# Two of a kernel's first loads issued from ScalarE's queue, and the constants issued behind the third k-tile

## The chip, the cores and the metric

The kernel runs on one core of a Trainium2 chip. The metric is the device time of one execution in microseconds (us). Five engines run side by side: TensorE (PE; its weight loads are listed apart as PEld), VectorE (DVE), ScalarE (ACT), GpSimd (POOL) and SyncE (SP). Loads from the chip's memory into the tiles are carried out by 16 DMA engines; an instruction on some engine's queue issues each load, and in the kernel before all of them stand on SP's queue.

## The reference: what is computed

One decoder layer on 256 positions of width 1024, in float32. What matters here is its first step, a product of the input with one wide weight matrix:

```python
proj = x @ w_in[l]
q = proj[..., 0:a].reshape(bsz, s, N_HEADS, HEAD_DIM)
k = proj[..., a:2 * a].reshape(bsz, s, N_HEADS, HEAD_DIM)
v = proj[..., 2 * a:3 * a].reshape(bsz, s, N_HEADS, HEAD_DIM)
...
y_att = moba_attention(q, k, v) @ w_attn_out[l]
y_cnv = (gate_b * causal_dwconv(gate_c * h_in, conv_w_mix[l])) @ w_conv_out[l]
mix = (g_att * y_att + g_cnv * y_cnv) @ w_o[l]
x = layer_norm(DEEPNORM_ALPHA * x + mix, ln1_g[l], ln1_b[l])
u = causal_dwconv(x @ w_up[l], conv_w_ffn[l])
f = (jax.nn.silu(u[..., :D_FF]) * u[..., D_FF:]) @ w_down[l]
x = layer_norm(DEEPNORM_ALPHA * x + f, ln2_g[l], ln2_b[l])
```

With a = 512, q, k and v are the first 1536 columns of `proj`.

## The kernel before

**The weights come in chunks.** All matrices are packed on the host into one array, `wpack`, in the order in which they are used. A chunk is a tile of 128 partitions and up to 2048 columns, called `raw0`, `raw1` and so on. The first eight chunks are the eight k-tiles of the first product: k-tile k holds 128 rows of the transposed input (256 columns) and the same 128 rows of q's, k's and v's weights (512 columns each), 1792 columns in all, or 896 KB.

**The first two k-tiles are loaded in pieces** (line 53). The text calls them by the number of the tile and a letter:

- 0a is columns 0 to 512 of `raw0`: the input and the first half of q's weights, 256 KB.
- 0b is columns 512 to 1280: the second half of q's weights and all of k's, 384 KB.
- 0c is columns 1280 to 1792: v's weights, 256 KB.
- 1a is columns 0 to 768 of `raw1`: the input and all of q's weights, 384 KB.
- 1b is columns 768 to 1792: k's and v's weights, 512 KB.

All later chunks are loaded whole. `issue_dma(c)` issues every chunk up to c that isn't issued yet.

**The order is written out by hand.** Each engine runs its instructions in the order in which the program names them. On SP stand `issue_dma(1)` (the five pieces), then the load of `consts` (81 KB: positions, convolution taps and the norm's columns), then `issue_dma(EARLY - 1)` with whole chunks from `raw2` on. The first chunks have tiles of their own; from `raw7` on a load reuses a tile, and waits until that is read.

**Each product is made of three matmuls in float32r.** A chunk's piece, once loaded, is split into a high part (`wh`, a copy by ScalarE, helper line 258, or line 222 later) and a low part (`wl`, a subtraction by VectorE, lines 255, 259 and 236); the input is split in the same way into `xT`. TensorE then multiplies high by high, low by high and high by low. K-tile 0 begins with the first half of q's columns (`first_q`, line 676, matmuls of 256 columns), so that it needs 0a alone; then come the second half of q, then k (both from 0b) and v (from 0c); then q of k-tile 1 (from 1a), its k and v (from 1b), and so on. Ahead of it TensorE runs 31 matmuls on constants (`warm_up`). VectorE reads `consts` for the first time in `rope_tables` (line 325). `neghalf2`, a tile of one column, is allotted at line 283; before its first real use it only receives one ACTIVATE at line 1003, far behind.

Of the kernel before, what the change touches and what calls it, by code (L numbers as in the profile page):

```python
# [8 lines left out]
F32 = mybir.dt.float32  # L9
# [4 lines left out]
AF = mybir.ActivationFunctionType  # L14
ALU = mybir.AluOpType

P = 128
# [33 lines left out]
CHUNK = 2048  # L51

PIECES = {0: (0, 512, 1280, 1792), 1: (0, 768, 1792)}
OFF_B, OFF_C, OFF_H, OFF_G = 3 * AW, 3 * AW + CW, 3 * AW + 2 * CW, 3 * AW + 3 * CW
TAIL = 8

# [73 lines left out]
def transfers(chunks, units):  # L130

    out, at = [], 0
    for c, us in enumerate(chunks):
        end = units[us[-1]][1] + units[us[-1]][2] * units[us[-1]][3]
        cuts = PIECES.get(c, (0, end))
        assert cuts[-1] == end
# [8 lines left out]
def layer_kernel(ctx: ExitStack, tc: tile.TileContext, x, wpack, cpack, b_gate, ln1_g, ln1_b, ln2_g, ln2_b, out):  # L145
    nc = tc.nc

    cst = ctx.enter_context(tc.tile_pool(name="cst", bufs=1))
# [8 lines left out]
    def acc_bank(name):  # L157
        return psum.tile([P, 512], F32, tag="acc", name=name)
# [20 lines left out]
    def issue_dma(c):  # L179
        nonlocal ln2  # L180
        while len(raws) <= c and len(raws) < len(chunks):
            i = len(raws)
            if i in RAW_HOMES:
                t = big.tile([P, CHUNK], F32, tag=RAW_HOMES[i], name=f"raw{i}")
            else:
                t = wp.tile([P, CHUNK], F32, tag="raw", name=f"raw{i}", bufs=RAW_BUFS)
            raws.append(t)
            for a, b, off in blocks[i]:
                nc.sync.dma_start(t[:, a:b], wpack[off:off + P * (b - a)].rearrange("(p n) -> p n", p=P))
            if i == LN2_CHUNK:  # L190
                ln2 = big.tile([P, 2, D], F32, tag="e8", name="ln2")
                for j, g in enumerate((ln2_g, ln2_b)):
                    nc.sync.dma_start(ln2[:, j, :], bass.AP(tensor=g.tensor, offset=g.offset, ap=[[0, P], [1, D]]))
# [19 lines left out]
    def split_start(u):  # L213
        issue_dma(units[u]["chunk"] + RAW_BUFS - 1)
        alloc(u, "h", "wh")
        alloc(u, "l", "wl")
        return units[u]["h"], units[u]["l"]

    def split_h(u):
        issue_dma(units[u]["chunk"] + RAW_BUFS - 1)  # L220
        alloc(u, "h", "wh")
        nc.scalar.activation(units[u]["h"], raw_of(u), AF.Copy)  # L222
# [36 lines left out]
        (eng or nc.vector).tensor_tensor(l, src, h.bitcast(F32), op=ALU.subtract)  # L259


    issue_dma(1)
    warm = acc_bank("warm")

# [15 lines left out]
    PCOL = [slice(0, 128), slice(128, 384)]  # L280
    neghalf = cst.tile([P, 1], F32, name="neghalf")
    nc.gpsimd.memset(neghalf, -0.5)
    neghalf2 = cst.tile([P, 1], F32, name="neghalf2")
    invf = cst.tile([P, 8], F32, name="invf")
    for i, f in enumerate(INV_FREQ):
        nc.gpsimd.memset(invf[:, i:i + 1], f)


    consts = cst.tile([P, 162], F32, name="consts")
    nc.sync.dma_start(consts, cpack)  # L290
    posi = consts[:, 144:146].bitcast(I32)
# [1045 lines left out]
    for k in range(TAIL):  # L1337
        i = NP - TAIL + k
# [116 lines left out]
```

## Time and profile before

| What | us |
|---|---|
| Median of 3 runs (lowest 350.74, highest 351.62) | 351.54 |
| The profiled execution's own time | 350.94 |
| Its span, first to last instruction | 349.2 |
| PE busy | 342.3 (98%) |
| DVE busy | 300.8 (86%) |
| ACT busy | 256.3 (73%) |
| POOL busy | 7.8 (2%) |

Busy times are those of the profiled execution, shares are of its span. The chain of work that ended last is 94% PE.

### The profile page before, as it was taken

Reading aid. Unit: us, or ns where it says so; the run is one execution under the profiler, and the core shown is the slowest. Engines: PE = TensorE matmul, PEld = TensorE weight load, DVE = VectorE, ACT = ScalarE, POOL = GpSimd, SP = SyncE. Lnnn points to the kernel's source line nnn. Section 1 sums busy time; section 2 is a strip of 40 time slices with the busy share of each in tenths; the row PEclk is TensorE's granted clock in tenths of the full one; section 3 lists DMA queues with packets and bytes.
Section 4 is the critical chain, followed back from the end, with each engine's and each line's share of the span. In section 5 each row is a group of like instructions: output and inputs, shape, how many; then the busy total and the mean of one; then the engine's idle time right before and its main releaser. Section 6 shows DMA issues by size and latency. Waiting matters only on the chain.

```text
span 349.2 us, 4612 instructions
## 1 busy us (share of the span) xinstructions
PE 342.3 (98%) x1577; PEld 283.9 (81%) x1577; DVE 300.8 (86%) x528; ACT 256.3 (73%) x396; POOL 7.8 (2%) x27
## 2 busy tenths in 40 slices
PE   9999999999999999999999999999999999999993
PEld 7888888888888888888888888888888888888882
DVE  4897759999998999799879999899799969597975
ACT  4776979599987857779786788977688867677600
POOL 1000002010000000000000000000000000000001
PEclk9999999999999999999999999999999999999999
DMA  7995985896848787993599759886887867795003
GB/s 267 424 396 207 237 285 206 127 330 206 276 103 349 282 315 213 289 343 97 134 353 237 233 190 213 238 315 160 293 282 266 280 179 261 178 374 154 0 16 105
DMA packets 58343, 82.17 MB, mean 235 GB/s; under 512 B 47824, under 2 KB 48336, under 8 KB 51280
## 3 DMA queue, kind: packets, MB, share of 16 engines
q1 hardware_dynamic: 58320, 81.88, 74.3%
q8 instruction: 12, 0.20, 0.2%
q14 instruction: 11, 0.09, 0.1%
HBM read 69.29 MB, written 1.05 MB: 201 GB/s over the span
## 4 chain that ended last, share of the span: by engine, by line
PE 94%; DVE 1%; DMA 1%; SPq 1%; issue 1%; POOL 0%; POOLq 0%; DVEq 0%; ACT 0%
PE u L342 10%; PE u L341 10%; PE u L340 10%; PE qk L660 6%; PE d L342 5%; PE d L341 5%; PE d L340 5%; PE g L340 4%; PE g L341 4%; PE g L342 4%; PE u L1198 3%; PE v L660 3%; PE y L340 2%; PE y L342 2%; PE y L341 2%; PE o L340 2%
## 5 line engine op out<-in xcount | busy, mean ns | idle before, releaser
L236 DVE TENSOR_TENSOR wl<-raw,wh 128x1024 fp32r<-128x1024 f32 x98 | 117.1, 1220 | 13.1 <-ACT wh L222 12.8
L222 ACT ACTIVATE wh<-raw 128x1024 fp32r<-128x1024 f32 x92 | 93.5, 1052 | 9.3 <-DMA raw<-in_wpack 9.3
L340 PE MATMUL u<-wh,x1T 128*128 128x512 f32 x160 | 62.2, 389 | 0.0
L341 PE MATMUL u<-wl,x1T 128*128 128x512 f32 x160 | 62.2, 389 | 0.0
L342 PE MATMUL u<-wh,x1T 128*128 128x512 f32 x160 | 62.2, 389 | 0.0
L341 PEld LDWEIGHTS u<-wl,x1T 128*128 128x128 f32 x160 | 30.0, 188 | 6.3
L340 PEld LDWEIGHTS u<-wh,x1T 128*128 128x128 f32 x160 | 30.0, 188 | 6.3
L342 PEld LDWEIGHTS u<-wh,x1T 128*128 128x128 f32 x160 | 30.0, 188 | 6.2
L1072 ACT ACTIVATE fc<-pb,consts 128x256 f32<-128x256 f32 x44 | 19.9, 499 | 14.0 <-DVE pb L1118 14.0
L341 PE MATMUL d<-wl,f 128*128 128x512 f32 x76 | 29.6, 389 | 0.0
L1106 ACT ACTIVATE up<-u 128x1024 uint16<-128x1024 uint16 x22 | 21.3, 1014 | 9.8 <-PE u L342 9.8
L259 DVE TENSOR_TENSOR wl<-raw,wh 128x1024 fp32r<-128x1024 f32 (+2 forms) x26 | 23.5, 944 | 3.6 <-ACT wh L258 3.5
L340 PE MATMUL d<-wh,f 128*128 128x512 f32 x68 | 26.5, 389 | 0.0
L342 PE MATMUL d<-wh,f 128*128 128x512 f32 x68 | 26.5, 389 | 0.0
L258 ACT ACTIVATE wh<-raw 128x1024 fp32r<-128x1024 f32 (+2 forms) x26 | 20.3, 828 | 7.0 <-DMA raw<-in_wpack 7.0
L340 PE MATMUL g<-wh,xT 128*128 128x512 f32 x64 | 24.9, 390 | 0.0
L341 PE MATMUL g<-wl,xT 128*128 128x512 f32 x64 | 24.9, 390 | 0.0
L342 PE MATMUL g<-wh,xT 128*128 128x512 f32 x64 | 24.9, 389 | 0.0
L1080 DVE SCALAR_TENSOR_TENSOR fc<-pb,consts,fc 128x254 f32<-128x254 f32 x44 | 21.3, 483 | 1.6
L1078 DVE SCALAR_TENSOR_TENSOR fc<-pb,consts,fc 128x255 f32<-128x255 f32 x44 | 21.1, 479 | 0.0
L660 PE MATMUL qk<-wh,xT 128*128 128x512 f32 x60 | 18.8, 392 | 0.0
L341 PEld LDWEIGHTS d<-wl,f 128*128 128x128 f32 x76 | 14.3, 188 | 3.0
(232 smaller groups left out, 655.9 us busy)
## 6 DMA issues: line engine op xcount, KB each, us to landing
raw<-in_wpack SPq DMA_DIRECT2D x55, 1024.0 KB, 5.3
raw<-in_wpack SPq DMA_DIRECT2D x6, 896.0 KB, 12.1
gb<-in_b_gate SPq DMA_DIRECT2D x4, 256.0 KB, 5.7
xr<-in_x SPq DMA_DIRECT2D x1, 1024.0 KB, 7.4
ln<-in_ln_g SPq DMA_DIRECT2D x2, 512.0 KB, 5.3
ln<-in_ln_b SPq DMA_DIRECT2D x2, 512.0 KB, 6.0
raw<-in_wpack SPq DMA_DIRECT2D x2, 384.0 KB, 4.6
raw<-in_wpack SPq DMA_DIRECT2D x2, 256.0 KB, 3.2
```

Source lines behind the costliest of these rows:

```text
L222: nc.scalar.activation(units[u]["h"], raw_of(u), AF.Copy)
L236: (eng or nc.vector).tensor_tensor(units[u]["l"], raw_of(u), units[u]["h"].bitcast(F32), op=ALU.subtract)
L258: nc.scalar.activation(h, src, AF.Copy)
L259: (eng or nc.vector).tensor_tensor(l, src, h.bitcast(F32), op=ALU.subtract)
L340: nc.tensor.matmul(o, ah, bh, start=start, stop=False)
L341: nc.tensor.matmul(o, ah, bl, start=False, stop=False)
L342: nc.tensor.matmul(o, al, bh, start=False, stop=stop)
L660: nc.tensor.matmul(banks[m][t], (xl if p == 2 else xh)[:, k, t * P:(t + 1) * P], wl if p == 1 else wh, start=k == 0 and p == 0, stop=k == ...
L1072: nc.scalar.activation(PB["c", i][a], PB[i][:, a * S:(a + 1) * S], AF.Copy, scale=w_ffn(2, j))
L1078: nc.vector.scalar_tensor_tensor(c[:, 1:S], pb[:, a * S:a * S + S - 1], w_ffn(1, j), c[:, 1:S], op0=ALU.mult, op1=ALU.add)
L1080: nc.vector.scalar_tensor_tensor(c[:, 2:S], pb[:, a * S:a * S + S - 2], w_ffn(0, j), c[:, 2:S], op0=ALU.mult, op1=ALU.add)
L1106: nc.scalar.activation(half.rearrange("p (w n) -> p w n", w=2), PB["rows", c][t].bitcast(U16).rearrange("p (n w) -> p w n", w=2), AF.Copy)
```

## The change

ScalarE gets an ACTIVATE on `neghalf2` at the very start, and behind it the issues of 0c and 1b, which leave SP's queue. The load of `consts` moves behind that of `raw2`.

```diff
 PIECES = {0: (0, 512, 1280, 1792), 1: (0, 768, 1792)}
+SIDE = ((0, 1280), (1, 768))
...
             for a, b, off in blocks[i]:
-                nc.sync.dma_start(t[:, a:b], wpack[off:off + P * (b - a)].rearrange("(p n) -> p n", p=P))
+                (nc.scalar if (i, a) in SIDE else nc.sync).dma_start(t[:, a:b], wpack[off:off + P * (b - a)].rearrange("(p n) -> p n", p=P))
...
+    ones = nc.const_aps.tensor(1.0, (P, 1), F32)
+    neghalf2 = cst.tile([P, 1], F32, name="neghalf2")
+    nc.scalar.activation(neghalf2, ones, AF.Copy)
     issue_dma(1)
     warm = acc_bank("warm")
...
     nc.gpsimd.memset(neghalf, -0.5)
-    neghalf2 = cst.tile([P, 1], F32, name="neghalf2")
     invf = cst.tile([P, 8], F32, name="invf")
...
+    issue_dma(2)
     consts = cst.tile([P, 162], F32, name="consts")
     nc.sync.dma_start(consts, cpack)
```

On SP's queue, at the start of the program, this stands in the kernel before (the number behind a tile's name is the program's own):

```order
L189 DMA raw0_76<-in_wpack 128x512
L189 DMA raw0_76<-in_wpack 128x768
L189 DMA raw0_76<-in_wpack 128x512
L189 DMA raw1_80<-in_wpack 128x768
L189 DMA raw1_80<-in_wpack 128x1024
L290 DMA consts_137<-in_cpack 128x162
L189 DMA raw2_147<-in_wpack 128x1792
L189 DMA raw3_151<-in_wpack 128x1792
```

and this in the changed one:

```order
L190 DMA raw0_78<-in_wpack 128x512
L190 DMA raw0_78<-in_wpack 128x768
L190 DMA raw1_82<-in_wpack 128x768
L190 DMA raw2_138<-in_wpack 128x1792
L294 DMA consts_140<-in_cpack 128x162
L190 DMA raw3_152<-in_wpack 128x1792
```

1a has moved from the fourth place to the third and `raw2` from the seventh to the fourth; 0c (128x512 of `raw0`) and 1b (128x1024 of `raw1`) are gone from here.

On ACT's queue, at the same place, the kernel before has the load of the function table and then the first copies:

```order
L680 ACT_TABLE_LOAD
L680 ACTIVATE xT_139<-raw0_76 128x256
L258 ACTIVATE wh1_149<-raw0_76 128x256
L258 ACTIVATE wh1_149<-raw0_76 128x512
L692 ACTIVATE wh2_185<-raw0_76 128x256
```

and the changed one has:

```order
L265 ACT_TABLE_LOAD
L265 ACTIVATE neghalf2_76<-const-float32-1.0 128x1
L190 DMA raw0_78<-in_wpack 128x512
L190 DMA raw1_82<-in_wpack 128x1024
L684 ACTIVATE xT_142<-raw0_78 128x256
L259 ACTIVATE wh1_150<-raw0_78 128x256
```

The two issues stand between the table load and the first copy of the input. On PE, DVE and POOL the order of instructions is the same in both kernels.

## Rows read from the trace of the kernel before

**Rows 1.** Busy time by stretch: PE first (count), PEclk, DMA share and GB/s last.

```profile
14.00:114.00 100.00, 100.00 (x480) 82.95 (x479) 87.67 (x175) 82.53 (x135) 3.32 (x4) 1.00 0.78 252
114.00:214.00 100.00, 100.00 (x442) 82.65 (x442) 91.60 (x144) 77.24 (x108) 1.17 (x2) 1.00 0.80 241
214.00:314.00 100.00, 100.00 (x443) 82.81 (x442) 87.26 (x136) 76.57 (x115) 0.00 (x0) 1.00 0.81 258
314.00:333.50 19.50, 19.50 (x87) 16.15 (x87) 15.10 (x33) 12.97 (x29) 0.00 (x0) 1.00 0.26 74
```

**Rows 2.** The chain that ended last, 0 to 16 us: start, length, what.

```profile
0.74 2.81 DMA raw<-in_wpack
...
8.80 2.98 PE qk L660 x12
...
13.14 2.72 PE qk L660 x12
```

**Rows 3.** Timeline of PE, 3.9 to 16 us: start, length, instructions merged.

```profile
3.73 0.22 PE L268 MATMUL warm<-const-bfloat16-1.0 128*128 128x128 bf16 x1
4.04 0.96 PE L676 MATMUL qk<-wh,xT 128*128 128x256 f32 x4
...
5.17 0.64 PE L676 MATMUL qk<-wh,xT 128*128 128x256 f32 x4
...
5.89 1.09 PE L660 MATMUL qk<-wh,xT 128*128 128x512 f32 x4
...
8.76 1.20 PE L660 MATMUL qk<-wh,xT 128*128 128x512 f32 x4
...
12.98 1.07 PE L660 MATMUL qk<-wh,xT 128*128 128x512 f32 x4
```

**Rows 4.** Timeline of the weight loads, 8 to 9.2 us; brackets: idle before, releaser.

```profile
8.76 0.53 PEld L660 LDWEIGHTS qk<-wh,xT 128*128 128x128 f32 x3 [0.38 <-ACT wh L258]
```

**Rows 5.** Timeline of ACT, 0 to 16 us.

```profile
0.73 1.28 ACT L680 ACT_TABLE_LOAD   x1 [0.73 <-PEq L1445]
3.57 0.42 ACT L680 ACTIVATE xT<-raw 128x256 fp32r<-128x256 f32 x1 [1.55 <-DMA raw<-in_wpack]
4.51 0.94 ACT L258 ACTIVATE wh<-raw 128x256 fp32r<-128x256 f32 x2 [0.52 <-DMA raw<-in_wpack]
5.35 0.40 ACT L692 ACTIVATE wh<-raw 128x256 fp32r<-128x256 f32 x1
8.07 0.63 ACT L258 ACTIVATE wh<-raw 128x512 fp32r<-128x512 f32 x1 [2.32 <-DMA raw<-in_wpack]
9.30 1.15 ACT L258 ACTIVATE wh<-raw 128x512 fp32r<-128x512 f32 x2 [0.59 <-DMA raw<-in_wpack]
11.68 1.68 ACT L258 ACTIVATE wh<-raw 128x512 fp32r<-128x512 f32 x3 [1.23 <-DMA raw<-in_wpack]
```

**Rows 6.** Busy time by stretch, 4 to 10 us, columns as in rows 1.

```profile
4.00:6.00 2.00, 1.96 (x13) 1.76 (x14) 1.71 (x4) 1.24 (x3) 0.00 (x0) 1.00 0.99 279
6.00:8.00 2.00, 2.00 (x11) 1.63 (x10) 1.07 (x3) 0.00 (x0) 0.00 (x0) 1.00 0.99 389
8.00:10.00 2.00, 2.00 (x9) 1.39 (x8) 1.36 (x4) 1.33 (x3) 0.00 (x0) 1.00 1.04 430
```

**Rows 7.** SP's timeline from 0 us, and line 189 up to 3.1 us (ns).

```profile
0.74 2.29 SPq L189 DMA_DIRECT2D raw<-in_wpack  x5
...
L189 SPq DMA_DIRECT2D raw<-in_wpack x5: 392/424/432, 0.7 to 2.6; - x5
```

**Rows 8.** Line 258 from 25.6 to 26 us: ns min/median/max, starts.

```profile
L258 ACTq EVENT_SEMAPHORE  x3: 17/17/17, 25.7 to 25.9; - x3
L258 ACT ACTIVATE wh<-raw x1: 1063/1063/1063, 25.6 to 25.6; 128x1024 fp32r<-128x1024 f32 x1
```

**Rows 9.** The first reader of the constants, and the smallest ACTIVATE before 26 us.

```profile
L325 DVE CAST posf<-consts x1: 164/164/164, 19.2 to 19.2; 128x2 f32<-128x2 int32 x1
...
24.21 0.23 ACT L314 ACTIVATE cs<-rrem 128x32 f32<-128x32 f32 x1
```

## The prediction

> **What bounds the kernel now.** I read the busy time by stretch first. From 14 to 333.5 us PE is busy in all of every stretch [rows 1], and the profile gives its matmuls no wait in there. So whatever happens at the start is carried, unchanged in size, to the end: a delay of TensorE there is a delay of the kernel, and time can be won only where TensorE stands still in the first 13 us. The chain of work shows where that is. It begins with the load of 0a (0.74 to 3.55 us), goes through ScalarE's first copy and stays on PE from 4.04 us on [rows 2, 3].
>
> In those 13 us three losses can be counted. First, TensorE starts at 4.04 us, while its last warm-up matmul starts at 3.73 us [rows 3]: 0.31 us at most. Second, q and k of k-tile 1 take 2.98 us for 12 matmuls, those of the next tile 2.72 us [rows 2]: 0.26 us lost, and the weight load ahead of them stood 0.38 us waiting for ScalarE's copy [rows 4], which itself began when 1a had landed, at 8.07 us [rows 5]. Third, the 12 short matmuls of q in k-tile 0 run from 4.04 to 5.89 us [rows 3], 1.85 us, where 12 of half of 2.72/12 us would need 1.36: 0.49 us. That last one is the chain of splits on ScalarE and VectorE, which the change leaves alone. The most that the head can give back is therefore 0.31 + 0.26 = 0.57 us.
>
> Then I read when loads land, from the copies on ACT that wait for them [rows 5]: 0a at 3.57 us, 0b at 4.51, 0c by 5.35 (its copy had no wait), 1a at 8.07, 1b at 9.30, raw2 at 11.68. And whether the DMA engines have room: from 4 to 10 us their share is 0.99 to 1.04, at 279, 389 and 430 GB/s [rows 6]. They are full. SP needs 2.29 us for its five issues, 0.39 to 0.43 each [rows 7], and runs well ahead of the landings.
>
> **The change, part by part.** *The ACTIVATE on neghalf2.* It brings the table load with it, which ACT does at 0.73 to 2.01 us anyway; a small ACTIVATE takes 0.23 us [rows 9]. ACT is idle until 3.57 us [rows 5], so 2.01 + 0.23 = 2.24 leaves 1.33 us of cover: nothing.
>
> *Two issues on ACT.* Of issues on ACT's queue no row shows any; SP's take 0.43 [rows 7]. Two of them behind 2.24 us end at 3.10, before the first copy at 3.57: nothing. What is queued behind them is that copy, and TensorE's first matmul behind it; were the two to take 0.67 us each or more, every further bit would be lost time. One row tells when they are issued: while a copy of 1063 ns ran from 25.6 us, ACT's queue went through three waits at 25.7 to 25.9 us [rows 8]. The queue runs ahead of the engine. So the issues need not wait for the table load, and may stand beside SP's first, at 0.8 us. I keep both ends, 0.8 and 2.24 us.
>
> *Fewer issues on SP.* 1a moves up one issue, raw2 three; at 2.29/5 = 0.46 us for each, 1a is issued 0.46 us sooner. In full DMA engines that alone moves no byte sooner. If landing followed issue, 1a would come at 7.61 us and the 0.26 us of k-tile 1 would go; that is the lower end.
>
> *The order of the bytes.* This is the term that counts. Before, one queue brought 0a, 0b, 0c, 1a, 1b in the order of use. Now 0c and 1b come on a queue of their own beside 0b and 1a. The bytes are the same, and the engines are full, so what 1b gets before 1a is finished delays 1a. Bounds from rows: if nothing of 1b goes ahead, 1a lands at 8.07 us as now; if all of it does, 1a is the last of the same bytes, and lands when 1b lands now, at 9.30 us [rows 5]. TensorE's k-tile 1 hangs on that landing directly, since it waits for it already [rows 4]: 0 to +1.23 us. I take the middle, +0.62 us: two queues that each get a share, the ends being one that gets none and one that gets all.
>
> For 0b the same: its first copy takes 0.42 us and TensorE begins the second half of q at 5.17 us [rows 3, 5]; 4.51 + 0.42 + 0.05 (the step from the first copy's end at 3.99 to the matmul at 4.04) = 4.98, so 0.19 us are in hand, and 0.26 us more because the wait at k-tile 1 absorbs them. 256 KB of 0c ahead of it cost 0.67 us at 389 GB/s and 0.94 at 279: +0.22 to +0.49 us at the end. This and 1a's delay aren't added: time lost in k-tile 0 is time in which 1a lands. The larger counts, so +0.62.
>
> *raw2 and the constants.* raw2 has only the 81 KB of consts less ahead of it. It lands at 11.68 and is needed at 12.98 us [rows 3, 5], less 0.63 us for a copy: 0.67 us in hand. Later tiles come no later than before. consts is read first at 19.2 us [rows 9], against raw2's landing at 11.68 just ahead of it: nothing.
>
> **A rule weighed.** The rows show a DMA share of 0.99 to 1.04 while the loads of the first k-tiles move [rows 6], so a load that is issued sooner finds no idle engine. The Trainium skill (DMA: Bandwidth & Descriptors, Issuing engines are not separate DMA queues) says that loads from several engines end up on the same 16 DMA engines and interleave, and that only the sequencer's time to issue is saved. By that saving alone, with nothing delayed, the sum would be -0.26 us; by the rows, with the order of the bytes counted, it is +0.62.
>
> **The sum.** The profiled execution took 350.94 us (span 349.2, and 1.74 around it); 350.94 + 0.62 = 351.56. The median of the three runs is 0.60 above the profiled one, so the forecast is 351.54 + 0.62 = 352.2 us. A difference of 0.3%, 1.05 us, is about what a measurement here tells from none.
>
> **The rivals.**
>
> *Slower by more than that.* If the issues on ACT run beside SP's first, 0c shares the engines with 0a and 0b, and then 1b with 0b. With 0c's 256 KB and an equal 384 KB of 1b before 0b is finished, 0b is late by 0.67 + 1.01 = 1.68 us at 389 GB/s (2.35 at 279). Less the 0.45 us in hand: +1.23 to +1.90 us, 352.8 to 353.4. 1a wholly behind 1b gives +1.23 too. It decides from the point where 0b lands later than 4.51 + 0.45 + 1.05 = 6.01 us, or 1a later than 9.12. For it speaks the queue that runs ahead [rows 8]; against it, that a queue with an issue of 0.46 us lead may keep the lead. The Trainium skill's page Perfetto Trace Analysis (DVE / Act Engine Instruction) has the sequencer push an instruction into a wait queue and go on; the three waits during a copy agree, and by it this rival is the result. I give it 0.33.
>
> *ACT's first copy is late.* If the issues wait for the engine and each takes over 0.67 us, the first copy begins after 3.57 us. At SP's price doubled, 2.24 + 4 x 0.43 = 3.96: +0.39 us, 351.9. Nothing shows such a price: 0.08.
>
> *Nothing lost, or a little won.* If SP's queue keeps its lead, or the pause between 4 and 6 us (279 GB/s against 389) is filled by a second queue, 1a lands before 7.8 us and the 0.26 us go: 351.3; with an earlier start of TensorE up to 0.57 us: 351.0. Both are within 0.3%. Faster than that would need a head that is worse in the timed runs than in the profiled one; their spread of 0.88 us leaves it open. 0.19 in all, 0.05 of it for faster by more than 0.3%.
>
> *The forecast:* 0.40.
>
> **How the numbers follow.** Faster 0.05. Slower: the first rival's 0.33, and 0.02 of the forecast's own upper end. Same: the rest, 0.60. The range reaches down to 351.0, all of the head's idle time given back, and up to 353.3, most of the first rival's. The forecast's own range, 1a from a quarter to four fifths behind 1b, is 351.8 to 352.5.
>
> **What would show it.** The issues of 0c and 1b on ACT's queue, at 0.8 to 1.3 us or at 2.2 to 2.7. ACT's copy of 1a's weights beginning between 8.1 and 9.3 us instead of 8.07, and the second half of q at or after 5.17 us. The copy of 1b's weights following 1a's without a wait. q of k-tile 2 at 12.98 + 0.62 = 13.6 us, and from there on the same intervals. The first matmul at 4.04 us if 0a is left alone; later if 0c shares its time. The prediction is wrong if 1a's copy begins before 8 us, if the first matmul moves by over 0.3 us, or if time moves behind 14 us.

## The result, and the profile after

The changed kernel takes 354.01 us (median of 6 runs, 353.33 to 354.11), the kernel before 351.25 (6 runs, 350.74 to 351.62): ratio 1.0078, 95% interval 1.0067 to 1.0089. It is 2.76 us slower, where +0.62 was forecast: the forecast of 352.2 with a range to 353.3 was wrong. The profiled execution took 354.03 us, with a span of 352.2, 3.0 us longer than before (349.2).

The busy time by stretch (PE first, PEclk, DMA share and GB/s last), beside [rows 1], shows where the time is not:

```profile
14.00:34.00 20.00, 20.00 (x90) 16.57 (x89) 17.47 (x35) 13.34 (x19) 0.00 (x0) 1.00 0.78 308
34.00:114.00 80.00, 80.00 (x392) 66.33 (x391) 66.78 (x137) 66.54 (x112) 3.10 (x4) 1.00 0.80 225
114.00:214.00 100.00, 100.00 (x443) 82.65 (x442) 91.52 (x142) 75.66 (x105) 1.17 (x2) 1.00 0.79 248
```

PE is as full as before, here and on to 336.5 us, so the 3 us are lost ahead of that, in the head. ACT's timeline up to 10 us, beside [rows 5]:

```profile
0.73 1.28 ACT L265 ACT_TABLE_LOAD   x1 [0.73 <-PEq L1449]
0.79 0.86 ACTq L190 DMA_DIRECT2D raw<-in_wpack  x2
2.02 0.20 ACT L265 ACTIVATE neghalf<-const-float32-1.0 128x1 f32<-128x1 f32 x1
4.40 0.42 ACT L684 ACTIVATE xT<-raw 128x256 fp32r<-128x256 f32 x1 [2.17 <-DMA raw<-in_wpack]
6.41 0.93 ACT L259 ACTIVATE wh<-raw 128x256 fp32r<-128x256 f32 x2 [1.60 <-DMA raw<-in_wpack]
...
7.86 1.67 ACT L259 ACTIVATE wh<-raw 128x512 fp32r<-128x512 f32 x3 [0.21 <-DMA raw<-in_wpack]
```

The two issues run at 0.79 to 1.65 us, while the engine still loads its table: ACT's queue did run ahead of the engine. 0a's copy comes at 4.40 us instead of 3.57, 0b's at 6.41 instead of 4.51. The copies of 1a and 1b at 7.86 us run on without a wait between them, where before they came at 8.07 and 9.30. PE's timeline, beside [rows 3]:

```profile
3.18 1.06 PE L272 MATMUL warm<-const-bfloat16-1.0 128*128 128x128 bf16 x8
4.87 1.25 PE L680 MATMUL qk<-wh,xT 128*128 128x256 f32 x4 [0.63 <-ACT xT L684]
...
6.88 1.22 PE L680 MATMUL qk<-wh,xT 128*128 128x256 f32 x4 [0.33 <-ACT wh L259]
...
8.32 1.91 PE L664 MATMUL qk<-wh,xT 128*128 128x512 f32 x4
10.03 0.69 PE L664 MATMUL qk<-wl,xT 128*128 128x512 f32 x2
10.56 1.07 PE L664 MATMUL v<-wh,xT 128*128 128x512 f32 x4
11.47 0.61 PE L664 MATMUL v<-wl,xT 128*128 128x512 f32 x2
11.92 1.07 PE L664 MATMUL qk<-wh,xT 128*128 128x512 f32 x4
...
16.00 1.07 PE L664 MATMUL qk<-wh,xT 128*128 128x512 f32 x4
```

The first matmul is late by 0.83 us (4.87 against 4.04), the second half of q by 1.71 (6.88 against 5.17), k-tile 2 by 3.02 (16.00 against 12.98). Between the second half of q and k-tile 1 no load is waited for, and yet 1.45 us more are lost (11.92 - 8.76 = 3.16). The chain of work, beside [rows 2], shows how:

```profile
6.88 1.65 PE qk L680 x6
8.53 2.19 PE qk L664 x6
10.72 1.36 PE v L664 x6
12.08 2.72 PE qk L664 x12
```

Six matmuls of 512 columns take 2.19 us at 8.5 us and 1.36 us from 10.7 us on, of the same form on tiles of the same size. In the timeline four of them begin between 8.32 and 10.03 us, 0.43 us each, which is 1.2 columns per ns; the four that begin between 10.56 and 11.47 us take 0.23 us each. Nothing is waited for in either place, so this is read as TensorE's clock: at its lower level of 1.2 GHz until about 10 us, at 2.4 GHz after it. The column PEclk doesn't show it (it reads 1.00 in the head as well); in the head the intervals of the matmuls have to be read instead.

The clock was already behind that of the kernel before when TensorE began to wait. The last eight warm-up matmuls, from 3.18 us on, took 1.06 us here (above), and in the kernel before

```profile
3.18 0.77 PE L268 MATMUL warm<-const-bfloat16-1.0 128*128 128x128 bf16 x8
```

There the pace doubled at 3.5 us, from 0.107 us a matmul to 0.06; here it was still the lower one at the last of them, at 3.92 us, though TensorE had done the same work up to then.

### The profile page after: what moved, and what is told of

Read it like the earlier page. It is cut to its first block, busy times and chain, and to the rows that moved or that the text cites. A ratio compares the mean times of both kernels' runs of the same rounds, so it can differ in the third digit from the quotient of the medians.

```text
span 352.2 us, 4613 instructions
## 1 busy us (share of the span) xinstructions
PE 344.5 (98%) x1577; PEld 286.0 (81%) x1577; DVE 300.2 (85%) x528; ACT 256.6 (73%) x397; POOL 7.6 (2%) x27
## 4 chain that ended last, share of the span: by engine, by line
PE 94%; DMA 2%; DVE 1%; SPq 1%; issue 1%; POOL 0%; POOLq 0%; DVEq 0%; ACT 0%
PE u L344 10%; PE u L346 10%; PE u L345 10%; PE qk L664 6%; PE d L346 5%; PE d L344 5%; PE d L345 5%; PE g L344 4%; PE g L345 4%; PE g L346 4%; PE v L664 3%; PE u L1202 3%; PE y L344 2%; PE y L345 2%; PE y L346 2%; PE o L345 2%
```

## The experiments

After the result a theory of two terms stood: the loads on ACT's queue bring 0a and 0b late, for about 1.5 us, and TensorE, idle meanwhile, gets its full clock late, for about 1.6 more. Its rivals: the clock has nothing to do with the idle time; a second queue harms as such, whatever the order; the ACTIVATE or the constants have a part. Each ratio below is to runs of the kernel before from the same batch, whose medians go from 350.74 to 351.25 us; so the ratio, and not the time alone, compares two batches.

**All loads back on SP's queue, the rest of the change kept.**

```diff
-SIDE = ((0, 1280), (1, 768))
+SIDE = ()
```

> The changed kernel with 0c and 1b back on SP's queue; the early ACTIVATE and the constants behind raw2 stay. Theory (the loads on ACT's queue are the cause): the same as before, 351.0 to 351.6 us, first matmul at 4.0 us, 0b's copy at 4.5. Rival (the ACTIVATE or the place of the constants has a part): above 352 us.

Measured: 351.04 us, ratio to the kernel before 0.9992 (0.9982 to 1.0003); first copy at 3.44 us, 0b's at 4.49. The ACTIVATE and the constants cost nothing. The loads on ACT's queue are the cause.

**Only 0c on ACT's queue** (`SIDE = ((0, 1280),)`).

> Only 0c on ACT's queue. Theory (bytes beside 0a and 0b delay them, and the idle TensorE then stays at the lower clock): first copy at 4.4 us as in the changed kernel, 0b's copy at 5.2 (0c's 0.67 us ahead of it), 0.8 us lost by the loads and 0.5 to 1.6 more by the clock: 352.3 to 353.7 us. Rival (it takes both loads): not over 351.8 us.

Measured: 351.74 us, ratio 1.0026 (1.0009 to 1.0043); eight of ten runs lie from 351.54 to 351.87, two at 353.35 and 353.58. First copy at 4.47 us, 0b's at 5.68, and k-tile 2 late by 0.82 us in the profile, where the clock was up in time. The time is below the theory's range and in that of the rival, that it takes both loads. But 0c alone does bring 0a and 0b late, and the loads' part, 0.82 us, is as expected; what didn't come in eight runs of ten is the clock's. That the other two, some 1.7 us slower, are the clock's is an inference: neither was profiled.

**Only 1b on ACT's queue** (`SIDE = ((1, 768),)`).

> Only 1b on ACT's queue. Theory: 1b's 512 KB share the engines with 0a and 0b; first copy at 4.4 us, 0b's at 5.5 to 6.2, with the lower clock after it 352.5 to 354.0 us. Rival (1b goes past 0a unharmed, and only 0c harms): first copy at 3.6 us, 351.2 to 351.9 us.

Measured: 353.22 us, ratio 1.0047 (1.0029 to 1.0065); three of eight runs lie from 352.04 to 352.12, five from 352.95 to 353.77. First copy at 4.59 us, 0b's at 6.05. The rival falls: 1b alone delays 0a as much as both do, and 0b nearly as much. The profiled execution is one of the three. Its chain has six matmuls in 1.39 us where the changed kernel's took 2.19:

```profile
6.05 0.42 ACT wh L259
6.47 0.04 issue
6.52 0.98 PE qk L680 x6
7.50 1.39 PE qk L664 x6
```

So an execution with 0b nearly as late can still have the clock early. That the five slower runs, some 1.4 us above the three, had it late is inferred from their times; none of them was profiled.

**TensorE kept busy while it waits: 42 warm-up matmuls, and 14 more between the halves of q.**

```diff
-    warm_up(31)
+    warm_up(42)
...
     first_q(0, (1,))
+    warm_up(14)
```

> The changed kernel with 42 warm-up matmuls instead of 31, and 14 more between the first and the second half of q in k-tile 0, so that TensorE isn't idle while it waits. It leaves the loads as they are: first copy at 4.4 us, 0b's at 6.4. Theory (two terms, late loads 1.5 us and the lower clock 1.6 us): the clock is up before the second half of q, matmuls of 512 columns every 0.23 us from there on, 352.3 to 352.9 us. Rival (the clock has nothing to do with TensorE's idle time): 0.43 us for each up to 10 us, as in the changed kernel, 353.7 to 354.3 us.

Measured: 353.11 us, ratio 1.0058 (1.0041 to 1.0076); first copy at 4.15 us, 0b's at 6.24. Matmuls of 512 columns stood 0.23 us apart from 7.5 us on, as the theory has it. The warm-up matmuls, which read constants alone and wait for no load, change their pace too: they stand 0.107 us apart until 4.0 us and 0.06 from 4.2 us on. In the chain the first lot takes 0.10 us each, the second 0.06:

```profile
0.77 4.08 PE warm L272 x42
...
5.92 0.84 PE warm L272 x14
```

But the time is above the theory's range. The waits of PE name why:

```profile
PE o L345 <- DVE wl L237: 0.5, 1, 0.5
```

That is a wait at 152 us that no other of these kernels has: k-tile 2 is late by only 1.38 us, the end by 2.15. The next run was made for it.

**A smaller filling: 36 and 8.**

```diff
-    warm_up(31)
+    warm_up(36)
...
     first_q(0, (1,))
+    warm_up(8)
```

> The changed kernel with 36 warm-up matmuls and 8 between the halves of q: a smaller filling than the one before it, whose profile lost 0.75 us again at 152 us, in a wait of TensorE that neither the kernel before nor the changed one has. Theory (late loads cost 1.5 us, the clock the rest; the wait at 152 us goes with the number of TensorE's instructions): no such wait, 352.2 to 352.8 us where the clock is up by 6.9 us. Rival (the wait at 152 us goes with the late loads): 353.0 us or more with the wait.

Measured: 352.39 us, all four runs from 352.25 to 352.48, ratio 1.0039 (1.0025 to 1.0054). Without a wait at 152 us. Its chain:

```profile
6.33 0.42 ACT wh L259
6.75 0.04 issue
6.79 0.99 PE qk L680 x6
7.78 1.39 PE qk L664 x6
```

0b's copy begins at 6.33 us, nearly as late as in the changed kernel (6.41), and yet 1.62 us are back by the medians, 1.59 by the two profiles and 1.4 by the two ratios. Of that, 1.46 us stand in the twelve matmuls above: 0.99 and 1.39 us here, 1.65 and 2.19 there. What is still lost against the kernel before is the loads' part: 1.45 us in the profile. The rest of the changed kernel's loss is the clock's. What makes the wait at 152 us in the other filling, with 24 more TensorE instructions than this one, stays open.

**The kernel before with a short warm-up: 8 instead of 31.**

```diff
-    warm_up(31)
+    warm_up(8)
```

> The kernel before with 8 warm-up matmuls instead of 31, all loads as they were, so that TensorE is idle from about 1.7 us to 4.0. Theory (an idle TensorE ahead of its work costs the clock): first copy at 3.6 us, first matmul at 4.0, matmuls of 512 columns every 0.43 us until 7 to 10 us, 352.5 to 353.8 us. Rival (the late loads alone explain the changed kernel): 351.0 to 351.6 us.

Measured: 352.47 us (351.55 to 352.87), just under the theory's range and clear of the rival's, ratio 1.0034 (1.0020 to 1.0049); first copy at 3.51 us, 0b's at 4.64, as in the kernel before. The chain:

```profile
3.98 2.96 PE qk L676 x12
6.94 2.56 PE qk L660 x6
9.50 1.48 PE v L660 x6
10.98 2.74 PE qk L660 x12
```

No load that TensorE waits for is late by more than 0.13 us and the first matmul starts as early as ever, but the first twelve matmuls take 2.96 us and the next two sixes 2.56 and 1.48, where they took 2.02, 1.39 and 1.36 in the kernel before. The clock alone costs 1.93 us in this profile, that of the slowest of the nine runs; by the ratio of all it is 1.2. The rival, that late loads explain everything, falls.

**0c and 1b issued on ACT's queue behind the first copy.** The two issues are put off until the copy of 0a's input.

```diff
     issue_dma(EARLY - 1)
     nc.scalar.activation(xh[:, 0, :], raws[0][:, 0:S], AF.Copy)
+    for dst, src in side:
+        nc.scalar.dma_start(dst, src)
```

> The changed kernel with the issues of 0c and 1b on ACT's queue behind the first copy, which waits for 0a. Theory: 0a is alone again, first copy at 3.6 us, first matmul at 4.0 with the clock up; 0b nearly alone, its copy at 4.5 to 4.8; 0c lands after 5.5 and 1b after 9, beside raw2: 351.0 to 352.0 us. Rival (a second queue harms as such): 353 us or more. If the queue runs ahead of the copy's wait, it is the changed kernel again, 354.0.

Measured: 354.98 us, ratio 1.0114 (1.0097 to 1.0132), the slowest of all. ACT's timeline:

```profile
3.43 0.42 ACT L688 ACTIVATE xT<-raw 128x256 fp32r<-128x256 f32 x1 [1.20 <-DMA raw<-in_wpack]
3.44 0.92 ACTq L690 DMA_DIRECT2D raw<-in_wpack  x2
4.53 0.94 ACT L263 ACTIVATE wh<-raw 128x256 fp32r<-128x256 f32 x2 [0.69 <-DMA raw<-in_wpack]
10.05 0.42 ACT L702 ACTIVATE wh<-raw 128x256 fp32r<-128x256 f32 x1 [4.59 <-DMA raw<-in_wpack]
10.38 0.61 ACT L263 ACTIVATE wh<-raw 128x512 fp32r<-128x512 f32 x1
13.52 2.72 ACT L263 ACTIVATE wh<-raw 128x512 fp32r<-128x512 f32 x5 [2.53 <-DMA raw<-in_wpack]
```

0a and 0b come in time, as expected; but 0c, issued at 3.44 us, is copied at 10.05, and 1b at 13.52. Behind 1a SP's queue holds raw2 and more, and with 0c and 1b issued later than these, TensorE waits for v of k-tile 0 and for k of k-tile 1. Of the bytes on ACT's queue none moved from 4 to 7 us. The expected range was wrong: 0c was thought of as landing beside 1a. The time lies in the range of the rival, that a second queue harms as such; but the harm is to the loads on that queue, and not, as in the changed kernel, to 0a and 0b.

**The loads reversed on SP's queue alone: 0a, 0c, 0b, 1b, 1a.**

```diff
-            for a, b, off in blocks[i]:
+            for a, b, off in (blocks[i][0], *blocks[i][:0:-1]) if i == 0 else blocks[i][::-1]:
```

> The kernel before with all five loads on SP's queue in the order 0a, 0c, 0b, 1b, 1a: the worst order of bytes that ACT's queue can bring, without a second queue and without touching 0a. Theory (order of bytes): first copy at 3.6 us, 0b's at 5.2, 1a's at 9.3; TensorE stands for 0.5 us at 0b and in all 1.0 to 1.5 us are lost: 352.2 to 352.8 us, more if the clock falls. Rival (the order is harmless, the second queue harms): 351.0 to 351.8 us.

Measured: 353.16 us (351.71 to 355.46), ratio 1.0068 (1.0037 to 1.0099). First copy at 3.51 us, as expected; 0b's at 6.12 instead of the expected 5.2, and 1a's at 8.98. The stretch from 4 to 6 us has part of the reason:

```profile
4.00:6.00 2.00, 1.66 (x9) 1.37 (x6) 0.72 (x2) 0.00 (x0) 0.00 (x0) 1.00 0.69 238
```

The engines moved only 238 GB/s there, as they moved only 279 in the kernel before [rows 6]: a slow stretch that falls on whatever load is under way. And the clock is late here too, behind TensorE's wait for 0b:

```profile
8.23 2.12 PE qk L660 x6
```

So the order of the loads harms without a second queue too, by late loads and by the clock; the rival falls. Two of the eight runs lie above 355.4 us, and what they lost is open.

**All loads on SP's queue, with longer warm-ups: 36 and 44.** They were to make the early rise of the clock likelier than in the kernel before.

> All loads on SP's queue, the constants behind raw2, 36 warm-up matmuls instead of 31, so that TensorE stays busy until the first copy is made. Theory (the spread of 350.5 to 351.6 us in the kernel before is that of the clock's rise, and a filled wait makes an early rise likelier): median 350.6 to 350.9 us. Rival (the spread has another cause): 350.9 to 351.3 us, as with 31.

> The same with 44 warm-up matmuls. At 0.107 us each they end after 5.4 us if the clock isn't up by then, after 4.6 us if it rises at 3.5: the first matmul is late by 0.5 to 1.4 us. Theory: the gain by the clock is smaller than that, 351.2 to 352.0 us. Rival (more warm-up always pays): under 350.9 us.

Measured: 351.24 us, ratio 1.0008 (0.9999 to 1.0016), and 351.41, ratio 1.0013 (1.0003 to 1.0022). Nothing is won with 36; the rival's range has it, though what spreads the runs isn't settled by that: in its profile the pace of the matmuls doubled only at 6.1 us, with 44 at 4.2. 44 costs about what was expected at the lower end.

**1b alone on ACT's queue, behind the first copy.**

> The changed kernel with 0c back on SP's queue in its old place, and 1b alone on ACT's, issued behind the first copy, which waits for 0a. Theory (a load on the second queue harms only the loads that are needed before it, and fills the engines' pause between 4 and 6 us): first copy at 3.5 us, 0b's at 4.5, 0c and 1a undisturbed, 1a before 8 us, 1b before 10 us; k-tile 1 without a wait; 350.6 to 351.2 us, not told from the kernel before. Rival (in the late issue of both loads it was 1b that harmed, and it is starved beside raw2's larger packets): 1b's copy at 12 us or later, TensorE stands at k of k-tile 1, 352.5 us or more.

Measured: 352.45 us, ratio 1.0033 (1.0020 to 1.0046). ACT's timeline:

```profile
3.44 0.41 ACTq L690 DMA_DIRECT2D raw<-in_wpack  x1
...
7.43 0.63 ACT L263 ACTIVATE wh<-raw 128x512 fp32r<-128x512 f32 x1 [0.79 <-DMA raw<-in_wpack]
10.99 2.72 ACT L263 ACTIVATE wh<-raw 128x512 fp32r<-128x512 f32 x5 [2.93 <-DMA raw<-in_wpack]
```

0a, 0b and 1a aren't harmed (1a's copy at 7.43 us; with all loads on SP's queue it came at 7.36), but 1b's comes only at 10.99, and TensorE's k of k-tile 1 waits until 11.67 us. The theory's range is missed. The rival named the place, but had 1b's copy at 12 us or later and the time a little higher. Of 1b, issued at 3.44 us, nothing moved before 6 us. No version was found that beats the kernel before.

## Why the prediction was wrong

**The step that failed first is the order of the bytes.** The forecast took 1a as the term that counts, "the middle, +0.62 us", and 0b as +0.22 to +0.49. It was 0b, of which the forecast had counted 0c's bytes ahead and none of 1b's: its copy came 1.90 us late, past the point of 6.01 us from which the first rival decides. 0a, the load that TensorE needs first, had no price at all, and its copy came 0.83 us late. The first rival was right in its mechanism and in its price for the loads: 0b late by 1.68 to 2.35 us was written, 1.90 measured; +1.23 to +1.90 us at the end, 1.45 measured with the clock's part taken out. It had 0.33, the forecast 0.40. The row that spoke for it was in hand: ACT's queue going ahead of a running copy [rows 8]. It holds for work under way: in the two kernels with late issues the queue did not go past an ACTIVATE that waited for its load. The reason given against it, that SP's queue keeps its lead of 0.46 us, had no row at all.

**The bounds on 1a were wrong as well.** 1a was to land between 8.07 and 9.30 us, since "the engines are full". It was copied at 7.86, and 1b with it. The lower bound was one execution's: in four other profiles with the loads on SP's queue in the old order the copy of 1a begins at 7.36, 7.83, 8.19 and 8.30 us, so a copy before 8 us told nothing of the second queue. And a DMA share of 0.99 was read as full; but at 279 GB/s from 4 to 6 us [rows 6] the engines could do more. With the second queue they moved half as much again:

```profile
4.00:6.00 2.00, 1.37 (x8) 1.14 (x6) 1.06 (x3) 0.42 (x1) 0.00 (x0) 1.00 1.04 422
```

The rival "Nothing lost, or a little won" had seen that the pause could be filled. It was, and it was worth nothing: 0a and 0b, the loads that TensorE needs first, paid for it. K-tile 1's wait of 0.26 us did go (2.72 us in the chain), but it is also gone with all loads on SP's queue.

**The step that was missing is TensorE's clock.** The prediction counted a late load as time in which TensorE stands, and nothing for how fast it runs afterwards. All six runs of the changed kernel (353.33 us or more) are slower than all four of the filled one (352.48 or less), whose 0b comes nearly as late, by 1.62 us in the median; the kernel before, with 8 warm-up matmuls and loads in time, loses 1.93 us in its profile. These two show that idle time ahead of the work costs the clock. It doesn't do so in every execution: in the profiles with 0c alone and with 1b alone TensorE waited 0.70 and 0.87 us for 0a, and its first matmuls had the higher pace all the same. What decides that is open. With this term the upper end of the first rival, and of the range, would have been some 1.5 us higher.

**What was right:** behind the head nothing changed (3.02 us late at k-tile 2, 3.0 at the end). The ACTIVATE was hidden (2.02 to 2.22 us, first copy at 4.40); the issues on ACT took 0.86 us and delayed no copy; the move of the constants cost nothing, as the run with all loads on SP shows. The wait of TensorE's first matmul for 0a was named as the sign against the forecast, "if the first matmul moves by over 0.3 us": it moved by 0.83.

**The rule that was weighed** (the Trainium skill, DMA: Bandwidth & Descriptors, Issuing engines are not separate DMA queues) says that loads from two queues interleave on the same engines. 0a's and 0b's delays, 0.83 and 1.90 us, agree with that. Its other half, that only issue time is saved, does not cover this case: 422 GB/s against 279 in the same stretch, though no time at the end.

## What to carry to other kernels

Where loads are issued in the order of use and TensorE follows close behind, a second queue takes that order away: a load that is needed later, issued at the start beside one that is needed now, delays it. Issued later, it left the earlier ones alone, but came late itself, behind what the first queue already held. No placement tried here beat one queue in the order of use. And when TensorE's first work moves back, move its warm-up with it, or count the lower clock: here that was as much as the late loads themselves.

## What the runs showed of the hardware

- ACT's queue issued loads at 0.79 us while the engine was in its table load until 2.01; but where an ACTIVATE ahead of the issue waited for a load, the issue came only when that had landed (3.44 us in both late kernels). In these runs it went ahead of work, not of waits. Issues on SP and ACT at the same time did not lengthen each other: 0.38 to 0.45 us each.
- From 4 to 6 us the loads moved 223 to 321 GB/s in the six kernels with SP's queue alone (279 in the kernel before), and 408 to 422 in the five with loads issued on ACT's queue at the start. Where ACT's loads were issued behind the first copy it was 271 and 284, and ACT's queue moved nothing in that stretch. Why is open.
- A load on the second queue that is issued late is served late: 256 KB took 6.6 us from issue to landing and 512 KB 9.6 (7.5 without the 256 KB), where the same pieces, issued at the start, took 3.8 and 6.1. How the engines divide their turns between two queues wasn't settled.
- When TensorE's pace doubled differs from execution to execution. In the eight profiles in which it had no wait between its first warm-up matmul and that time, it was at 3.5 us (the kernel before) to 6.8. In three with a wait ahead of it, the changed kernel, the reversed order and the short warm-up, it was at 9.6 to 10.2 us; in two others, with 0c alone and 1b alone, it was doubled at the first matmul, at 4.9 and 5.1. What decides between early and late wasn't settled.
